# Moving the pool branch of each pass's first block into the key/query stage, with later group projections, spaced mix norms and held-back x loads

## The chip, the cores and the metric

The kernel runs as one program on all 8 cores of one Trainium2 chip (two dies of four cores). Each core computes 2048 tokens of a sequence and recomputes a halo block of 512 tokens in front of them. The time of a run is the device time of the slowest core, in microseconds (us). The four fast runs of the kernel before lie within 0.2% (1667.71 to 1671.0 us). Some executions fall into a slower state, in which the cores of one die, sometimes of both, show a lower mean granted TensorE clock: 0.81 to 0.93 in the slow runs, against 0.968 to 0.995 in profiled fast runs. A median below is that of the fast runs. In the traces of the kernel before, the clock records hold full and half clock alone. Matmuls of 512 columns start 0.214 us apart in gapless stretches at full clock and 0.43 us apart at half clock.

In this document PE is TensorE, DVE is VectorE, ACT is ScalarE, POOL is GpSimd and SP is SyncE. L179, L185 and so on are lines of the kernel. They are the lines of small helpers, so one line stands for many operations:

- L179 matmul, L185 and L186 activation (without and with a bias operand);
- L189 tensor-tensor, L194 scalar-tensor-tensor, L196 the same with an accumulated sum;
- L201 tensor-scalar, L209 copy or cast, L212 memset, L215 load or store.

## The reference

A macaron block: a SwiGLU feed-forward network (FFN), a token mixer with two gated branches, and a second FFN. Shift, scale and gate of each come from a conditioning vector through `w_ada`.

```python
def token_mix(h, w_in, ...):
    z = h @ w_in
    q, k, v, u, ga, gb = jnp.split(z, ...)          # 512, 512, 512, 512, 1024, 1024 columns
    ya = chunk_band_attention(q, k, v, ...) @ w_attn_out   # RMS norm of q and k per head, 8 heads
    yb = multiscale_pool(u, w_group, scale) @ w_pool_out   # trailing means of 2, 4, 8, 16 frames
    return (sigmoid(ga) * ya + sigmoid(gb) * yb) @ w_o

def multiscale_pool(u, w_group, scale):
    ...                                             # per group g: trailing mean minus u itself
    y = einsum('bsgc,gcd->bsgd', mixed, w_group)    # the group projection, 128x128 per group
    return y * scale
```

## The kernel before

Each core handles five blocks of 512 tokens, block 0 being the halo. The order of stages is: start (norms of blocks 0 and 1, `w_ada` dots), first FFN, then twice (a pass for blocks 1 and 2, another for 3 and 4) a key/query stage, attention and gates, then the second FFN. Matmuls run at bf16; weight loads other than `w_ada` cast from f32 on the way and are issued by POOL. SP issues `w_ada` and x.

**The filler.** In the key/query and attention stages, matmuls use what ScalarE makes of earlier ones (squares, logarithms, exponentials). `Fill` holds generators of other matmul work, for PE to run meanwhile, and feeds them in by credit. With it, PE's waits for ScalarE come to 2.3 us in the first key/query stage and 1.5 us in the first attention pass (core 4 of the kernel before). One credit is about one matmul of 512 columns.

```python
class Fill:
    def later(self, n, fn):            # run fn when n more credits of fill have passed
        self.late.append([n, fn])
    def run(self, n):
        self.credit += n
        while self.gens and self.credit > 0:
            try:
                c = next(self.gens[0]); self.credit -= c; self._passed(c)
            except StopIteration:
                self.gens.popleft()
        ...
```

**The fill work.** A value job has four tiles of 8 matmuls with two casts each. A pool job has four groups. Each group is 8 matmuls, a copy, 1 to 4 shifted adds on VectorE, and a subtraction. The group projection (one matmul and a scale, `yp`) comes 10 credits later. Both jobs take turns in two PSUM banks through `fbank`.

```python
    def fbank():
        fb[0] += 1
        return bank(4 + fb[0] % 2)

    def v_job(b, pas):
        for t in range(4):
            bk = fbank()
            ...                                        # 8 matmuls, yield 2 after each pair
            for o in range(2): ... P.copy(dst, src[:, :, o, :])        # L209, VectorE
            yield 2

    def u_job(b, pas, fill, in_a):
        def yp(g):
            bk = fbank()
            P.mm(bk, WPG[:, g, :], MIXED[g % 3][:, :], True, True)
            P.ts(yb_[:, g, :], bk, CST[:, 106 + g:107 + g], ALU.mult)  # L201, VectorE
        for g in range(4):
            bk = fbank()
            ...                                        # 8 matmuls
            u = UB[g % 2]
            if in_a: P.act(u[:, 16:528], bk, AF.Copy)  # first block of the pass: ScalarE
            else:    P.copy(u[:, 16:528], bk)          # second block: VectorE
            yield 2
            for st in range(g + 1):
                P.tt(dst[:, lo:528], src[:, lo:528], src[:, lo - sh:528 - sh], ALU.add)
                yield 0.5
            P.stt(MIXED[g % 3][:, :], src[:, 16:528], 1.0 / (2 << g), u[:, 16:528], ALU.mult, ALU.subtract)
            ...
            fill.later(10, lambda g=g: yp(g))
            yield 0.5
```

**The schedule.** `kq_seq(items, pas, fill, lead)` makes keys or queries: per half item, 16 matmuls, a square on ScalarE, `fill.run(lead)`, two matmuls for the head norms, then Ln, Exp and one VectorE operation. `attention(pas, fill, rate)` makes 40 steps (8 groups of 5, each group ending in a softmax denominator) and runs about `rate` credits of fill per step, less two for each value product.

```python
        if pas == 0:
            fill.add(v_job(0, pas))
            kq_seq([("K", 0)], pas, fill, 6)
            for t in tl: t.drain()                     # what is left of the mix norms
            fill.add(v_job(1, pas))
            kq_seq([("K", 1), ("Q", 1)], pas, fill, 6)
            kq_seq([("K", 2)], pas, fill, 6)
            release(("K", 0, pas), ("K", 1, pas))      # loads the U weights
            fill.add(u_tail(pas))
            fill.add(u_job(b1, pas, fill, True))
            kq_seq([("Q", 2)], pas, fill, 6)
        else: ...                                      # v_job(3), K3 K4, u_job(3), Q3 Q4, leads of 6
        fill.run(6)
        fill.add(v_job(b2, pas))
        fill.add(u_job(b2, pas, fill, False))
        attention(pas, fill, 5.0)
```

**The tail of the first FFN** (its last output projection) makes the mix norms of blocks 0 to 2. `tail_1(b, n)` is called after each of four output projections of a block and steps a queue of norm groups after three of them.

**The start.** SP queues x of blocks 2 to 4 (2 MB each) right behind the start's `w_ada` loads. POOL loads the first FFN's w1i pieces when certain `w_ada` dots are done. The first unit of four (a unit is 16 matmuls: one 128-column slice of the hidden layer for one block) overlaps the dots.

## Time and profile before

The median before was 1668.5 us (1667.71 to 1671.0 in three runs). The profiled execution spans 1667.4 us on its slowest core, core 4.

First the page. The lines of part 2 cut the span into 40 slices of about 42 us, and each digit is a busy share in tenths. PEclk is the granted clock in tenths of full speed.

```profile
PE 1537.1 (92%) x7085; PEld 672.7 (40%) x7085; DVE 820.2 (49%) x1300; ACT 480.2 (29%) x615; POOL 95.7 (6%) x191
...
PE   1498999999999998898799998799999999999999
...
PEclk9799999999999998898899998799999999999999
...
PE 83%; DVE 5%; ACT 4%; DMA 4%; issue 3%; SPq 0%; DVEq 0%; ACTq 0%; POOL 0%
```

PE is the limit, and the chain of waits that ends last is 83% PE. So only stretches where PE is not at 9 can be gained. These are the start, slices 16 and 17 (the end of the first FFN), and slices 19, 20, 25 and 26, which hold the attention stages.

Next PE's waits in total (us, times, longest).

```profile
PE ps L179 <- ACT arena L185: 37.1, 23, 11.9
PE ps L179 <- ACT arena L186: 27.3, 9, 14.6
PE ps L179 <- DMA arena<-w1i: 16.0, 3, 6.8
PE ps L179 <- DVE arena L209: 15.6, 7, 4.1
PE ps L179 <- DVE arena L194: 14.4, 6, 4.1
PE ps L179 <- DVE arena L189: 7.8, 4, 3.4
PE ps L179 <- DVE arena L201: 6.9, 3, 3.3
```

The four DVE lines sum to 44.7 us, nearly all in the tail, key/query and attention stages.

Then PE's timeline at the start (start, length, instruction, and in brackets the idle time before it with what ended it).

```profile
59.94 0.59 PE L179 MATMUL ps<-arena 128*128 128x512 bf16 x2 [1.85 <-ACT arena L186]
65.26 3.41 PE L179 MATMUL ps<-arena 128*128 128x512 bf16 x8 [4.73 <-DMA arena<-w1i]
73.16 3.57 PE L179 MATMUL ps<-arena 128*128 128x512 bf16 x8 [4.49 <-DMA arena<-w1i]
83.49 21.79 PE L179 MATMUL ps<-arena 128*128 128x512 bf16 x88 [6.76 <-DMA arena<-w1i]
```

PE waits three times for w1i, whose loads share the DMA engines with 6 MB of x: on this core x lands at 63.1, 70.8 and 77.5 us, w1i at 65.1, 73.0 and 83.4 us, and the DMA engines' busy share from 60 to 80 us is 1.01.

In the tail, the same view shows waits for squares on ScalarE, and one that ends in VectorE. VectorE was itself waiting for the `w_ada` loads of its last dots (4.71, 0.40, 2.12 and 4.14 us, from 612.7 to 629.6 us).

```profile
632.60 19.84 PE L179 MATMUL ps<-arena 128*128 128x512 bf16 x78 [3.89 <-DVE arena L194]
654.38 0.59 PE L179 MATMUL ps<-arena 128*128 128x512 bf16 x2 [1.93 <-ACT arena L185]
...
670.70 1.53 PE L179 MATMUL ps<-arena 128*128 128x512 bf16 x3 [3.60 <-ACT arena L185]
```

In the first attention pass, every wait of note is for VectorE. (How its work stands in line: PE ended at 778.44 us, and the casts that it waited for began at 780.95, directly behind four operations of L189 that VectorE had itself begun only at 778.91, after 3.35 us of waiting for ScalarE.)

```profile
769.59 8.86 PE L179 MATMUL ps<-arena 128*128 128x512 bf16 x39 [3.35 <-DVE arena L189]
781.86 5.19 PE L179 MATMUL ps<-arena 128*128 128x512 bf16 x19 [3.41 <-DVE arena L209]
...
812.80 7.19 PE L179 MATMUL ps<-arena 128*128 128x512 bf16 x38 [3.27 <-DVE arena L201]
...
828.22 3.26 PE L179 MATMUL ps<-arena 128*128 128x512 bf16 x17 [4.15 <-DVE arena L194]
```

Last, the busy time by window for the first key/query stage (first line) and the first attention pass (second line). The columns are window and length, busy us of PE, PEld, DVE, ACT and POOL with their instruction counts, then granted clock, DMA share and GB/s.

```profile
688.10:747.70 59.60, 56.52 (x279) 24.40 (x276) 26.88 (x48) 34.64 (x36) 2.82 (x4) 0.97 0.19 30
747.70:837.30 89.60, 68.24 (x363) 25.25 (x362) 56.71 (x130) 54.25 (x67) 8.50 (x36) 0.85 0.04 6
```

In attention no engine is full, and the granted clock is 0.85: PE keeps stopping, and stretches at half clock follow (0.43 us from one matmul to the next, as at 771 us). In the key/query stage PE is nearly full.

### The profile page before, as it was taken

To read this page: it belongs to the slowest core of one execution; us is meant where nothing else is said; L and a number is where in the kernel's file an instruction comes from. 1 tells how busy PE (TensorE), PEld (TensorE's weight loads), DVE (VectorE), ACT (ScalarE), POOL (GpSimd) and SP (SyncE) were. 2 spreads that over 40 slices of the span, in tenths; PEclk is the share of its full clock that TensorE was granted. 3 is DMA by queue.
4 is the path that set the end of the run, shared out by engine and by line. 5 is a ranking of instruction groups with operands and counts; after the bars stand their busy time and mean duration, and the time that the engine had idled before them with its cause. 6 is when DMAs were issued, how large, how long until landed. Compare 5 with 4: busy or idle time off the path is not lost.

```text
span 1667.4 us, 20421 instructions; the slowest of 8 cores (1653.6 to 1667.4 us)
## 1 busy us (share of the span) xinstructions
PE 1537.1 (92%) x7085; PEld 672.7 (40%) x7085; DVE 820.2 (49%) x1300; ACT 480.2 (29%) x615; POOL 95.7 (6%) x191
## 2 busy tenths in 40 slices
PE   1498999999999998898799998799999999999999
PEld 0133444444444443342244432244434444444444
DVE  4446736447346346735745445645456161613416
ACT  3354010110110114655644165644150101011110
POOL 0101000010010000000011100001101000001000
PEclk9799999999999998898899998799999999999999
DMA  9923353161370353030054530044504313104005
GB/s 280 267 54 88 62 123 80 39 140 33 90 145 10 89 127 75 1 51 1 1 89 76 88 51 1 1 89 77 88 1 76 51 26 57 26 14 83 13 1 202
DMA packets 45938, 119.50 MB, mean 72 GB/s; under 512 B 4112, under 2 KB 4240, under 8 KB 45328
## 3 DMA queue, kind: packets, MB, share of 16 engines
q0 software_dynamic: 31152, 59.91, 21.8%
q1 hardware_dynamic: 14688, 58.30, 10.7%
q8 instruction: 60, 0.98, 0.2%
q14 instruction: 38, 0.31, 0.1%
HBM read 169.70 MB, written 8.39 MB: 107 GB/s over the span
## 4 chain that ended last, share of the span: by engine, by line
PE 83%; DVE 5%; ACT 4%; DMA 4%; issue 3%; SPq 0%; DVEq 0%; ACTq 0%; POOL 0%
PE ps L179 83%; ACT arena L185 3%; DMA arena<-w_ada 2%; DVE arena L189 2%; DVE arena L194 2%; DMA arena<-w1i 1%; DVE arena L196 1%; ACT arena L186 1%; SPq L215 0%; DVE arena L209 0%; ACT L185 0%; ACT L186 0%; DVE arena L201 0%; DVEq L173 0%; DVE arena L205 0%
## 5 line engine op out<-in xcount | busy, mean ns | idle before, releaser
L179 PE MATMUL ps<-arena 128*128 128x512 bf16 (+5 forms) x7085 | 1537.1, 380 | 126.4 <-ACT arena L185 37.1
L179 PEld LDWEIGHTS ps<-arena 128*128 128x128 bf16 (+1 forms) x7085 | 672.7, 99 | 990.3 <-issue 246.6
L185 ACT ACTIVATE arena<-ps 128x512 bf16<-128x512 f32 (+4 forms) x368 | 271.0, 745 | 911.1 <-PE ps L179 903.7
L189 DVE TENSOR_TENSOR arena<-arena,ps 128x512 bf16<-128x512 bf16 (+1 forms) x230 | 175.2, 762 | 560.8 <-PE ps L179 493.3
L194 DVE SCALAR_TENSOR_TENSOR arena<-ps,arena 128x512 f32<-128x512 f32 (+1 forms) x410 | 315.5, 774 | 155.3 <-PE ps L179 80.2
L185 ACT ACTIVATE arena<-arena 128x1024 bf16<-128x1024 f32 (+2 forms) x105 | 95.2, 929 | 37.5 <-PE ps L179 15.8
L196 DVE SCALAR_TENSOR_TENSOR arena<-arena 128x1024 f32<-128x1024 f32 x72 | 87.8, 1220 | 32.4 <-DMA arena<-w_ada 18.3
L189 DVE TENSOR_TENSOR arena<-arena 128x512 bf16<-128x512 bf16 (+9 forms) x191 | 89.9, 494 | 27.0 <-ACT arena L185 19.6
L186 ACT ACTIVATE arena<-arena 128x512 bf16<-128x512 f32 (+1 forms) x84 | 57.5, 715 | 124.8 <-DVE arena L194 103.1
L194 DVE SCALAR_TENSOR_TENSOR arena<-arena 128x512 f32<-128x512 f32 (+2 forms) x114 | 78.9, 728 | 1.9 <-ACT arena L186 0.5
L215 POOL DMA_DIRECT2D arena<-w1i x26 | 17.1, 660 | 520.0 <-PE ps L179 470.2
L189 DVE TENSOR_TENSOR arena<-ps,arena 64x512 bf16<-64x512 f32 x32 | 22.0, 688 | 43.4 <-ACT arena L185 43.0
L215 POOL DMA_DIRECT2D arena<-w3i x24 | 16.3, 678 | 380.3 <-PE ps L179 380.3
L215 POOL DMA_DIRECT2D arena<-w_in x28 | 19.8, 707 | 297.3 <-PE ps L179 297.3
L186 ACT ACTIVATE arena<-ps,arena 128x1024 f32<-128x1024 f32 (+1 forms) x32 | 29.6, 926 | 17.4 <-PE ps L179 17.2
L185 ACT ACT_TABLE_LOAD x14 | 18.0, 1283 | 43.7 <-PE ps L179 36.5
L201 DVE TENSOR_SCALAR arena<-arena 128x512 bf16<-128x512 f32 (+2 forms) x45 | 19.8, 441 | 6.0 <-DMA arena<-cst 1.0
L212 POOL MEMSET arena<- 64x128 bf16 x64 | 11.9, 198 | 166.8 <-ACT arena L185 166.8
L186 ACT ACT_TABLE_LOAD x12 | 15.4, 1283 | 13.4 <-PE ps L179 13.3
L201 DVE TENSOR_SCALAR arena<-ps,arena 128x512 bf16<-128x512 f32 (+2 forms) x25 | 15.6, 638 | 4.6 <-PE ps L179 4.4
L209 DVE CAST arena<-ps 128x256 bf16<-128x256 f32 x32 | 12.0, 418 | 4.3 <-PE ps L179 4.0
L215 POOL DMA_DIRECT2D arena<-w_o x8 | 5.6, 704 | 73.8 <-PE ps L179 73.8
(14 smaller groups left out, 51.5 us busy)
## 6 DMA issues: line engine op xcount, KB each, us to landing
arena<-w_ada SPq DMA_DIRECT2D x72, 512.0 KB, 4.3
arena<-w_in POOLq DMA_DIRECT2D x28, 512.0 KB, 6.1
arena<-w3i POOLq DMA_DIRECT2D x20, 512.0 KB, 6.3
arena<-w1i POOLq DMA_DIRECT2D x18, 512.0 KB, 10.0
outT<-arena SPq DMA_DIRECT2D x16, 512.0 KB, 3.0
arena<-xT SPq DMA_DIRECT2D x3, 2048.0 KB, 23.0
arena<-w1o POOLq DMA_DIRECT2D x10, 512.0 KB, 16.5
arena<-w3o POOLq DMA_DIRECT2D x10, 512.0 KB, 9.6
```

The source lines that it names most:

```text
L179: return self.op("pe", lambda e: e.matmul(out, lhsT=lhsT, rhs=rhs, start=start, stop=stop), reads=[lhsT, rhs], writes=[out])
L185: return self.op("act", lambda e: e.activation(out=out, in_=in_, func=func, scale=scale), r, [out])
L186: return self.op("act", lambda e: e.activation(out=out, in_=in_, func=func, bias=bias, scale=scale), r, [out])
L189: return self.op(eng, lambda e: e.tensor_tensor(out=out, in0=in0, in1=in1, op=op), [in0, in1], [out])
L194: return self.op("dve", lambda e: e.scalar_tensor_tensor(out=out, in0=in0, scalar=scalar, in1=in1, op0=op0, op1=op1), r, [out])
L196: return self.op("dve", lambda e: e.scalar_tensor_tensor(out=out, in0=in0, scalar=scalar, in1=in1, op0=op0, op1=op1, accum_out=accum), r, ...
L201: return self.op(eng, lambda e: e.tensor_scalar(out=out, in0=in0, scalar1=s1, scalar2=None, op0=op0), r, [out])
L209: return self.op(eng, lambda e: e.tensor_copy(out=out, in_=in_), [in_], [out])
L212: return self.op(eng, lambda e: e.memset(out, v), [], [out])
L215: return self.op(q, lambda e: e.dma_start(out=out, in_=in_), [], [out], deps, sem)
```

## The change

The intent has five parts:

1. Start: hold the x of blocks 2 to 4 back until the first FFN's second w1i chunk has landed, and issue the w1i pieces at earlier dots. Put the `w_ada` dots of the first group in its last three blocks.
2. Tail: step the norm queue after every output projection, with empty groups that space a norm's matmuls from its squares.
3. Key/query stage: do the whole pool branch of the pass's first block there, with larger leads. The U weights are loaded before the Q weights. In the first pass the norms of blocks 1 and 2 are stepped inside.
4. Group projections 30 credits behind instead of 10, with four mix buffers. The projection takes the bank that the next job will use, without advancing the counter.
5. Attention: rate 4 instead of 5. Value tiles and pool groups of the second block alternate.

```diff
-            fill.later(10, lambda g=g: yp(g))
+            fill.later(30, lambda g=g: yp(g))
 ...
-            bk = fbank()
-            P.mm(bk, WPG[:, g, :], MIXED[g % 3][:, :], True, True)
+            bk = bank(4 + (fb[0] + 1) % 2)
+            P.mm(bk, WPG[:, g, :], MIXED[g][:, :], True, True)
 ...                                                   # first pass
+            tl[0].drain()
             fill.add(v_job(0, pas))
-            kq_seq([("K", 0)], pas, fill, 6)
-            for t in tl: t.drain()
-            fill.add(v_job(1, pas))
-            kq_seq([("K", 1), ("Q", 1)], pas, fill, 6)
-            kq_seq([("K", 2)], pas, fill, 6)
-            release(("K", 0, pas), ("K", 1, pas))
+            kq_seq([("K", 0)], pas, fill, 10, hook)
+            tl[1].drain()
             fill.add(u_tail(pas))
             fill.add(u_job(b1, pas, fill, True))
-            kq_seq([("Q", 2)], pas, fill, 6)
+            fill.add(v_job(1, pas))
+            kq_seq([("K", 1)], pas, fill, 10, hook)
+            tl[2].drain()
+            kq_seq([("K", 2)], pas, fill, 11)
+            release(("K", 0, pas), ("K", 1, pas))
+            kq_seq([("Q", 1), ("Q", 2)], pas, fill, 11)
 ...                                                   # second pass: leads 9, v and u alternate
-        fill.run(6)
-        fill.add(v_job(b2, pas))
-        fill.add(u_job(b2, pas, fill, False))
-        attention(pas, fill, 5.0)
+        for k in range(4):
+            fill.add(u_job(b2, pas, fill, False, [k]) if k < 2 else v_job(b2, pas, [k]))
+            fill.add(v_job(b2, pas, [k]) if k < 2 else u_job(b2, pas, fill, False, [k]))
+        fill.run(10)
+        attention(pas, fill, 4.0)
 ...                                                   # tail
+        for t in tl: t.step()                          # now after all four n
+                for k in (2, 1): ng.insert(k, [])
 ...                                                   # start
-                      [(0, 1), (2, 3)], (4, 5), startup=[dots[2], dots[11]], ...
+                      [(0, 1), (2, 3)], (4, 5), startup=[dots[1], dots[7], dots[11], dots[13]], ...
+    last = pre1()
+    P.load("sp", XB[1][:, :, :], xT[2], "d_x2", deps=last)      # then w_ada, then x of blocks 3 and 4
```

More of the change, by code (lines that the diff above doesn't have):

```diff
@@ L365, in build_nc @@
     TT = [view(o_h + 2112, F32, (528,)), view(o_h + 4224, F32, (528,))]
-    MIXED = [view(o_h + 6336, BF16, (TB,)), view(o_w + 4096 * 9 + 2112, BF16, (TB,)), view(base - 4096, BF16, (TB,))]
+    MIXED = [view(o_h + 6336, BF16, (TB,)), view(o_w + 4096 * 9 + 2112, BF16, (TB,)), view(base - 4096, BF16, (TB,)),
+             view(base - 2048, BF16, (TB,))]
     SG = [view(o_h + 4096 * i, F32, (2, TB)) for i in range(2)]
@@ L523, in build_nc @@
             early(b, kt)
-    for i in range(2):
-        ada_load(16 + i, ada_slot(16 + i), "d_b%d" % i)
-    for b in range(2, 5):
-        P.load("sp", XB[b - 1][:, :, :], xT[b], "d_x%d" % b)
     ada_j = [16]
@@ L558, in wi_load @@
             if split is not None:
-                for jj in range(nt):
-                    for s, o in ((sa, 0), (sb, NJ)):
-                        P.load("pool", piece(s)[:, jj:jj + 1, :],
+                return [P.load("pool", piece(s)[:, jj:jj + 1, :],
                                w_i[o + j0 + jj:o + j0 + jj + 1].rearrange("j p c -> p j c"),
-                               "d_w%d" % s if jj == 0 else "d_wy%d" % s, deps=[split[jj]])
-                return
+                               "d_w%d" % s if jj == 0 else "d_wy%d" % s, deps=[split[2 * k + jj]])
+                        for jj in range(nt) for s, o in ((sa, 0), (sb, NJ))]
             for s, o in ((sa, 0), (sb, NJ)):
@@ L612, in pre @@
         def pre():
-            wi_load(startup)
+            return wi_load(startup)
         def body():
-            wi_load()
+            if startup is None:
+                wi_load()
             wo_load(0)
@@ L681, in g0_1 @@
         g0_norms(4 * bi + u, N1)
-        if bi >= 1 and u % 2 == 0:
+        if bi >= 2 and u < 3:
             ada_step()
@@ L697, in tail_1 @@
     def tail_1(b, n):
+        for t in tl:
+            t.step()
         if n == 6:
@@ L708, in tail_1 @@
                     ng.append([lambda: P.copy(HT[:, :, :], H[0][:, :, TB - 16:TB])])
+                for k in (2, 1):
+                    ng.insert(k, [])
                 tl[b].q.extend(ng)
-            return
-        for t in tl:
-            t.step()
     pre1, body1 = ffn(w1i, w1o, 0, [0, 1, 2, 3, 4], True, dict(g0=g0_1, g0end=g0end_1, unit=unit_1, op=lambda: None),
-                      [(0, 1), (2, 3)], (4, 5), startup=[dots[2], dots[11]], tail=tail_1,
+                      [(0, 1), (2, 3)], (4, 5), startup=[dots[1], dots[7], dots[11], dots[13]], tail=tail_1,
                       spread=lambda kt: warm(5) if 2 <= kt <= 6 else None)
     pre1()
+    last = pre1()
+    P.load("sp", XB[1][:, :, :], xT[2], "d_x2", deps=last)
+    for i in range(2):
+        ada_load(16 + i, ada_slot(16 + i), "d_b%d" % i)
+    for b in range(3, 5):
+        P.load("sp", XB[b - 1][:, :, :], xT[b], "d_x%d" % b)
     P.load("pool", WPG[:, :, :], w_pg.rearrange("(g c) d -> c g d", c=128), "d_wpg", deps=[dots[15]])
@@ L759, in build_nc @@
     for p_ in range(2):
-        for k in ("K", "V", "Q", "U"):
+        for k in ("K", "V", "U", "Q"):
             wq.extend([(k, 0, p_), (k, 1, p_)])
@@ L767, in build_nc, with kq_seq @@
     flag = CST[:, 110:111]
-    def kq_seq(items, pas, fill, lead):
+    def kq_seq(items, pas, fill, lead, hook=None):
         n_ = 0
@@ L780, in kq_seq @@
                 P.act(SQK[i], pair(i), AF.Square)
+                if hook is not None:
+                    hook()
                 fill.run(lead)
@@ L797, in fbank, with v_job @@
         return bank(4 + fb[0] % 2)
-    def v_job(b, pas):
+    def v_job(b, pas, tiles=range(4)):
         sl = SLOT[b]
-        for t in range(4):
+        for t in tiles:
             bk = fbank()
@@ L833, in u_tail, with u_job @@
         yield 4
-    def u_job(b, pas, fill, in_a):
+    def u_job(b, pas, fill, in_a, gs=range(4)):
         yb_ = YP[(b - 1) % 2]
         def yp(g):
-            bk = fbank()
-            P.mm(bk, WPG[:, g, :], MIXED[g % 3][:, :], True, True)
+            bk = bank(4 + (fb[0] + 1) % 2)
+            P.mm(bk, WPG[:, g, :], MIXED[g][:, :], True, True)
             P.ts(yb_[:, g, :], bk, CST[:, 106 + g:107 + g], ALU.mult)
-        for g in range(4):
+        for g in gs:
             bk = fbank()
@@ L864, in u_job @@
                 yield 0.5
-            P.stt(MIXED[g % 3][:, :], src[:, 16:528], 1.0 / (2 << g), u[:, 16:528], ALU.mult, ALU.subtract)
+            P.stt(MIXED[g][:, :], src[:, 16:528], 1.0 / (2 << g), u[:, 16:528], ALU.mult, ALU.subtract)
             if b == 1:
@@ L868, in u_job @@
                 P.tt(t16[:, 0:16], src[:, 16:32], CST[:, 112 + 16 * g:128 + 16 * g], ALU.mult)
-                P.tt(MIXED[g % 3][:, 0:16], t16[:, 0:16], u[:, 16:32], ALU.subtract)
-            fill.later(10, lambda g=g: yp(g))
+                P.tt(MIXED[g][:, 0:16], t16[:, 0:16], u[:, 16:32], ALU.subtract)
+            fill.later(30, lambda g=g: yp(g))
             yield 0.5
@@ L976, in build_nc, with hook @@
         if pas == 0:
-            v_ones(0)
-            fill.add(v_job(0, pas))
-            kq_seq([("K", 0)], pas, fill, 6)
-            for t in tl:
-                t.drain()
-            v_ones(1)
-            v_ones(2)
-            fill.add(v_job(1, pas))
-            kq_seq([("K", 1), ("Q", 1)], pas, fill, 6)
-            kq_seq([("K", 2)], pas, fill, 6)
-            release(("K", 0, pas), ("K", 1, pas))
+            def hook():
+                for t in tl[1:]:
+                    t.step(2)
+            tl[0].drain()
+            for b in range(3):
+                v_ones(b)
+            fill.add(v_job(0, pas))
+            kq_seq([("K", 0)], pas, fill, 10, hook)
+            tl[1].drain()
             fill.add(u_tail(pas))
             fill.add(u_job(b1, pas, fill, True))
-            kq_seq([("Q", 2)], pas, fill, 6)
+            fill.add(v_job(1, pas))
[4 more added lines that the diff above has]
+            kq_seq([("Q", 1), ("Q", 2)], pas, fill, 11)
         else:
@@ L993, in build_nc @@
             v_ones(4)
-            fill.add(v_job(3, pas))
-            kq_seq([("K", 3), ("K", 4)], pas, fill, 6)
+            for k in range(4):
+                fill.add(v_job(3, pas, [k]))
+                fill.add(u_job(b1, pas, fill, True, [k]))
+            kq_seq([("K", 3), ("K", 4)], pas, fill, 9)
             release(("K", 0, pas), ("K", 1, pas))
-            fill.add(u_job(b1, pas, fill, True))
-            kq_seq([("Q", 3), ("Q", 4)], pas, fill, 6)
+            kq_seq([("Q", 3), ("Q", 4)], pas, fill, 9)
         release(("Q", 0, pas), ("Q", 1, pas))
-        fill.run(6)
-        fill.add(v_job(b2, pas))
-        fill.add(u_job(b2, pas, fill, False))
-        attention(pas, fill, 5.0)
+        for k in range(4):
+            fill.add(u_job(b2, pas, fill, False, [k]) if k < 2 else v_job(b2, pas, [k]))
+            fill.add(v_job(b2, pas, [k]) if k < 2 else u_job(b2, pas, fill, False, [k]))
+        fill.run(10)
+        attention(pas, fill, 4.0)
         release(("V", 0, pas), ("V", 1, pas), ("U", 0, pas), ("U", 1, pas))
```

## The prediction

> **What bounds the kernel now.** TensorE. The page gives it 92% busy; its 7085 recorded matmuls, at the 0.214 us per 512-column matmul of the gapless stretches, fill at most 1464 us of the 1667 us span. The chain of waits is 83% PE. Stages where PE idles matter; in 20 us windows and PE's timeline:
>
> 1. Start: PE runs gaplessly only from 152 us. Units 2 to 4 of the first block wait for w1i (4.7, 4.5, 6.8 us); the last piece, issued at 59.5, lands at 83.4, behind 6 MB of x issued at 47 us. They also run at half clock (0.43 us per matmul).
> 2. End of the first FFN: DVE waits for the last w_ada dots (617 to 631 us); PE idles 3.9 us, then runs 16 matmuls at half clock.
> 3. The tail with mix norms (640 to 706 us): PE idles 1.9, 3.6, 0.8 and 2.3 us, mostly for squares, half clock following.
> 4. Attention, 748 to 838 and about 1000 to 1087 us. A group of five steps takes 13 us while pool-branch work fills it, 7.6 us with value-projection fill, 6.8 us without (denominators in ScalarE's timeline). PE there waits 2 to 4 us for VectorE (casts L209, scale L201, L189, L194). No engine is full; VectorE's in-order chain costs, with the group projection only 10 matmuls behind it.
>
> [...] Here gaps of 1.9 to 3.9 us are followed by 0.43 us matmuls, so a removed gap counts nearly double.
>
> **What the change does.** No arithmetic goes; work moves.
> - x loads wait for the second w1i chunk, which is issued at dots 11 and 13 (51 and 55 us), so should land near 61 us. Unit 4 starts near 68 us, not 83.5. Given back: the later blocks' x lands at 73 to 90, so ScalarE's squares stall a little. Net -12 us.
> - Ada dots leave the second block, three in each later block: neutral there, but the last comes one unit earlier: -5 us.
> - Spaced norm groups in the tail: -9 us of idle and slow clock.
> - First pass: about 50 fill matmuls move from attention into the key/query stage, gapless on PE from 707 to 748 us: +10.6 us there. Second pass: about 28, +6 us.
> - Attention: the fill falls from about 112 and 88 to 62 matmuls, pool groups alternate with value tiles, and the group projection comes 30 matmuls later. ScalarE then bounds it: 40 exponentials of 1.02 us (1.1 apart) plus eight denominators of 1.8 us, 58 us a pass. Expected: 65 to 68 us against 87 and 84: -21 and -17 us.
>
> Sum: -12 -5 -9 +10.6 +6 -21 -17 = -47; a little goes to new waits.
>
> **Predicted: 1623 us, 1604 to 1643 with 80%.** Faster by over 2%: 0.80; within 2%: 0.19; slower: 0.01.
>
> **Right if:** no PE wait for w1i near 83 us, and gapless PE begins near 140 us; no half-clock stretch at 632 us; key/query stages longer; attention groups of 7.5 to 9 us instead of 12 to 13; PE's waits for L209/L201/L194 nearly gone (30 us before).
>
> **Wrong if:** held-back x makes ScalarE hold up the SiLUs behind its squares, so the start gains little; query weights, now loaded only after key weights are released, arrive late; or attention stays bound by latency, PE at half clock for want of fill.

(The mark stands for a sentence that was cut, since nothing in this case shows the rule it gave for the clock. No term of the sum went with it: -12 -5 -9 +10.6 +6 -21 -17 = -47.4, put there as -47. That a removed gap counts nearly double is the author's estimate, from matmuls 0.43 us apart instead of 0.214 behind gaps of core 4. The landing times of w1i (61 us) and of the later x (73 to 90 us) are the author's estimates too, and so are the 1.1 us between exponentials: in the kernel before they start 0.90 us apart or more, for example at 792.23, 793.13, 794.03 and 795.21 us on core 4.)

## The result, and the profile after

The changed kernel took 1639.03 us in the median (1637.44 to 1643.42, four runs), against 1668.4 us before. The ratio is 0.9825 with a 95% interval of 0.9803 to 0.9847. A ratio is the mean time of one kernel's fast runs over that of the other's of the same rounds, so it is not quite the ratio of the quoted medians. The kernel is clearly faster, by 1.75%. That is short of the 2% which would count as "faster".

The page of the slowest core (core 3, span 1638.0 us):

```profile
PE 1517.3 (93%) x7085; PEld 669.1 (41%) x7085; DVE 821.3 (50%) x1300; ACT 478.9 (29%) x615; POOL 96.2 (6%) x193
...
PE   1488999999999999988699988799999999999999
...
PEclk9899999999999999999999999899999999999999
...
PE 82%; ACT 5%; DVE 5%; DMA 4%; issue 3%; SPq 0%; DVEq 0%; ACTq 0%; POOL 0%; POOLq 0%
```

PE's waits:

```profile
PE ps L179 <- ACT arena L185: 55.6, 35, 12.0
PE ps L179 <- ACT arena L186: 29.5, 10, 17.5
PE ps L179 <- DVE arena L201: 10.9, 5, 3.9
PE ps L179 <- DVE arena L209: 7.3, 4, 3.0
PE ps L179 <- DMA arena<-w_ap: 5.9, 2, 3.4
PE ps L179 <- DVE arena L189: 5.9, 6, 2.4
PE ps L179 <- DVE arena L194: 0.6, 1, 0.6
```

The waits for w1i are gone and the DVE waits fell from 44.7 to 24.7 us. The wait for the scale (L201) grew from 6.9 to 10.9 us, the wait for ScalarE (L185) grew by 18.5 us, and a wait for `w_ap` is new on this core. Where those new waits lie is visible in PE's timeline.

```profile
62.65 7.50 PE L179 MATMUL ps<-arena 128*128 128x512 bf16 x34 [0.83 <-ACT arena L186]
82.11 8.15 PE L179 MATMUL ps<-arena 128*128 128x512 bf16 x30 [11.96 <-ACT arena L185]
...
646.25 0.59 PE L179 MATMUL ps<-arena 128*128 128x512 bf16 x2 [2.75 <-ACT arena L185]
...
724.89 2.32 PE L179 MATMUL ps<-arena 128*128 128x512 bf16 x10 [3.24 <-DVE arena L201]
...
760.18 4.94 PE L179 MATMUL ps<-arena 128*128 128x512 bf16 x17 [3.04 <-DVE arena L209]
```

At the start there is one gap of 12 us on this core where there were three for w1i. ScalarE's timeline says what it was doing in that time:

```profile
66.64 1.08 ACT L185 ACTIVATE arena<-ps 128x512 bf16<-128x512 f32 x2
80.91 2.00 ACT L185 ACTIVATE arena<-arena 128x1024 bf16<-128x1024 f32 x2 [13.19 <-DMA arena<-xT]
82.82 0.58 ACT L185 ACTIVATE arena<-ps 128x512 bf16<-128x512 f32 x1
```

It stood before the squares of block 2, which need the held-back x. PE waits for these squares themselves: the norm statistics of block 2, four matmuls over squares, stand in PE's stream before the fourth unit. On all eight cores PE starts again 0.14 to 0.15 us after the first square ends. The SiLU of the third unit, whose matmuls had ended at 70.15, stood in line behind the squares too (the line at 82.82), but the fourth unit uses the PSUM pair of the first, whose SiLU had run at 66.64. (Some expectations below place this gap before the fifth unit; it lies before the fourth.)

The windows of the first key/query stage and the first attention pass:

```profile
672.50:743.90 71.40, 64.40 (x316) 28.39 (x314) 40.74 (x83) 36.98 (x40) 2.81 (x4) 0.98 0.20 30
743.90:812.50 68.60, 53.04 (x318) 20.23 (x318) 42.03 (x93) 51.64 (x63) 7.50 (x35) 0.93 0.00 1
```

The attention pass has 45 matmuls less (363 to 318), VectorE lost 14.7 us of work in it, and it took 68.6 us instead of 89.6. The key/query stage took 71.4 us instead of 59.6.

The slowest core differs from run to run, so the experiments below are read by stage, as means over all eight cores of each profile. The bounds in the first FFN are the ends of SiLUs on ScalarE, one for each unit: the 4th, the 20th (end of the first group) and the 110th (the last output projection follows). Matmuls can't be counted there, because two cores of before and two of after lack 140 matmul records in their traces. The later bounds are the first key matmul (taken as 3.6 us before the first square of keys), the first attention matmul, and the last narrow one. This table was worked out from the traces in that way.

| stage, mean of 8 cores, us | before | after | difference | predicted |
|---|---|---|---|---|
| to the end of the fourth unit | 91.1 | 82.4 | -8.7 | |
| rest of the first group | 71.6 | 73.0 | +1.4 | the two: -12 |
| rest of the first FFN | 457.3 | 457.3 | 0.0 | |
| tail | 59.9 | 55.7 | -4.2 | -5 and -9 |
| key/query stage, first pass | 59.1 | 71.4 | +12.3 | +10.6 |
| attention, first pass | 88.8 | 69.6 | -19.2 | -21 |
| gates, first pass | 114.5 | 114.9 | +0.4 | |
| key/query stage, second pass | 43.9 | 53.3 | +9.4 | +6 |
| attention, second pass | 89.7 | 67.1 | -22.6 | -17 |
| rest | 583.3 | 583.6 | +0.3 | |
| span | 1659.4 | 1628.4 | -31.0 | -47 |

The same traces say what the 31.0 us consist of. In the mean of the cores PE's idle time fell by 15.6 us (129.5 to 113.9), and the time in which PE ran at half clock fell by 30.7 us (72.9 to 42.2), which is 15.4 us of work at full clock.

The start is the least steady of these stages. In the runs whose start code is that of the change, the first group ends between 155.4 and 158.6 us (155.4 in the change's own profile), so differences of 3 us there say nothing.

### The profile page after: what moved, and what is told of

It reads as the page before. It is cut to its first block, busy times and chain, and to the rows that moved or that the text cites. A ratio compares the mean times of both kernels' runs of the same rounds, so it can differ in the third digit from the quotient of the medians.

```text
span 1638.0 us, 20449 instructions; the slowest of 8 cores (1622.4 to 1638.0 us)
## 1 busy us (share of the span) xinstructions
PE 1517.3 (93%) x7085; PEld 669.1 (41%) x7085; DVE 821.3 (50%) x1300; ACT 478.9 (29%) x615; POOL 96.2 (6%) x193
## 4 chain that ended last, share of the span: by engine, by line
PE 82%; ACT 5%; DVE 5%; DMA 4%; issue 3%; SPq 0%; DVEq 0%; ACTq 0%; POOL 0%; POOLq 0%
PE ps L179 82%; ACT arena L185 3%; DVE arena L189 2%; DVE arena L194 1%; DMA arena<-w_ada 1%; ACT arena L186 1%; DMA arena<-w_ap 1%; DMA arena<-xT 1%; DVE arena L196 1%; SPq L215 0%; DMA arena<-w1i 0%; DVE arena L209 0%; DVE arena L201 0%; ACT L185 0%; ACT L186 0%
## 5 line engine op out<-in xcount | busy, mean ns | idle before, releaser
L179 PE MATMUL ps<-arena 128*128 128x512 bf16 (+3 forms) x7085 | 1517.3, 377 | 116.8 <-ACT arena L185 55.6
L185 ACT ACTIVATE arena<-ps 128x512 bf16<-128x512 f32 (+4 forms) x368 | 270.3, 744 | 870.5 <-PE ps L179 862.1
L194 DVE SCALAR_TENSOR_TENSOR arena<-ps,arena 128x512 f32<-128x512 f32 (+1 forms) x410 | 315.8, 774 | 125.6 <-PE ps L179 71.1
L185 ACT ACTIVATE arena<-arena 128x1024 bf16<-128x1024 f32 (+2 forms) x105 | 95.2, 929 | 42.8 <-DMA arena<-xT 17.6
L189 DVE TENSOR_TENSOR arena<-arena 128x512 bf16<-128x512 bf16 (+10 forms) x191 | 89.9, 494 | 25.5 <-ACT arena L185 17.3
L194 DVE SCALAR_TENSOR_TENSOR arena<-arena 128x512 f32<-128x512 f32 (+2 forms) x114 | 78.8, 727 | 6.2 <-ACT arena L186 2.9
L201 DVE TENSOR_SCALAR arena<-arena 128x512 bf16<-128x512 f32 (+2 forms) x45 | 19.9, 443 | 5.7 <-DMA arena<-cst 1.1
L186 ACT ACT_TABLE_LOAD x12 | 15.4, 1283 | 16.3 <-PE ps L179 16.2
L201 DVE TENSOR_SCALAR arena<-ps,arena 128x512 bf16<-128x512 f32 (+2 forms) x25 | 15.7, 644 | 7.2 <-PE ps L179 7.0
L209 DVE CAST arena<-ps 128x256 bf16<-128x256 f32 x32 | 12.1, 419 | 7.4 <-PE ps L179 7.4
L209 DVE COPY arena<-arena 128x16 f32<-128x16 f32 (+2 forms) x35 | 6.0, 171 | 8.2 <-ACT arena L185 6.8
```

What stands on the lines that cost most here:

```text
L179: return self.op("pe", lambda e: e.matmul(out, lhsT=lhsT, rhs=rhs, start=start, stop=stop), reads=[lhsT, rhs], writes=[out])
L185: return self.op("act", lambda e: e.activation(out=out, in_=in_, func=func, scale=scale), r, [out])
L186: return self.op("act", lambda e: e.activation(out=out, in_=in_, func=func, bias=bias, scale=scale), r, [out])
L189: return self.op(eng, lambda e: e.tensor_tensor(out=out, in0=in0, in1=in1, op=op), [in0, in1], [out])
L194: return self.op("dve", lambda e: e.scalar_tensor_tensor(out=out, in0=in0, scalar=scalar, in1=in1, op0=op0, op1=op1), r, [out])
L201: return self.op(eng, lambda e: e.tensor_scalar(out=out, in0=in0, scalar1=s1, scalar2=None, op0=op0), r, [out])
```

## The experiments

All twelve kernels gave correct results. The runs of one call (1 to 4; 5 to 8; 9 to 11; 12) share their runs of the kernel before. Times of different calls come from different chips, so their ratios are compared as well.

### 1. The start put back

```diff
-    P.load("sp", XB[1][:, :, :], xT[2], "d_x2", deps=last)   # and the rest of the change's start
+    for b in range(2, 5):                                    # behind the last w_ada loads, as before
+        P.load("sp", XB[b - 1][:, :, :], xT[b], "d_x%d" % b)
-startup=[dots[1], dots[7], dots[11], dots[13]]
+startup=[dots[2], dots[11]]
-        if bi >= 2 and u < 3:
+        if bi >= 1 and u % 2 == 0:
```

> The change with its start put back: x loads, w1i pieces and ada dots as in the kernel before. Costing of the prediction: the start is worth 12 us (and 5 more at the end of the first FFN on the core that waited there), so 1651 to 1656 us. Reading of the two traces over all cores: the fourth unit starts 10.5 us earlier but the norms of the first group give 3.2 us back, so about 1646 us. Rival: on the slowest core the wait for w1i was only swapped for a wait for x (12 us for the squares), so no more than 4 us, 1640 to 1643 us.

Measured: 1647.15 us, ratio 0.9858 (0.9837 to 0.9879). The fourth unit is done at 93.4 us instead of 82.4 in the mean, and the first group at 165.7 instead of 155.4. The tail is 58.9 us in the mean instead of 55.7, because two cores stand at 65.5 and 67.1 us: the wait that VectorE ends (L194, behind the last `w_ada` dots) is back there with gaps of 6.64 and 6.88 us, and on no other core. The start is worth about 8 us in the time. That falls short of the prediction's costing (-12 and -5) and fits the reading over all cores (about 1646 us).

### 2. The tail put back as it was, without spacing

```diff
-        for t in tl:                    # at the head of tail_1
-            t.step()
-                for k in (2, 1):
-                    ng.insert(k, [])
+            return                      # no step after the fourth output projection
+        for t in tl:
+            t.step()
```

> The change with the mix norms of the tail stepped as in the kernel before (three groups per block, no empty ones). Costing of the prediction: the spacing is worth 9 us, so 1648 us, with gaps of 1.9 and 3.6 us before the norm matmuls and half-clock matmuls after them. Reading of the traces: the tail lost one gap of the two and kept one of 2.75 us, so 3 to 4 us, 1643 us. Rival: the gain there was the removed ada wait alone, so 1639 us.

Measured: 1639.59 us, ratio 0.9808 (0.9791 to 0.9825). The time is that of the change. By stage the tail is 58.7 us instead of 55.7, and the gaps of 1.93 and 3.60 us are back as expected. The key/query stage is 1.4 us longer and the following attention 1.7 us shorter. So the spacing removes about 3 us in the tail's own stage, and no gain in the time could be shown (the first group also ended 2.1 us later in this run, which is chance). The prediction's 9 us for it is wrong.

### 3. Projection early, everything else as changed

```diff
-            fill.later(30, lambda g=g: yp(g))
+            fill.later(10, lambda g=g: yp(g))
```

> The change with the group projection 10 matmuls behind its pool group instead of 30; all else as changed. Theory that lateness is what freed attention: groups with pool work go back to 11 to 13 us, each attention pass from 68 to about 80 us, time 1655 to 1662 us. Rival, that moving the first block's pool branch out and alternating pool groups with value tiles freed it: passes stay below 73 us, time 1639 to 1645 us.

Measured: 1657.08 us, ratio 0.9911 (0.9891 to 0.993). The time fell into the range of the first theory, but for another reason. The attention passes took 72.0 and 69.9 us, only 2.4 and 2.8 us more than with the change, so they stayed nearly free. The loss is in the key/query stages: 82.6 us instead of 71.4 and 56.3 instead of 53.3. PE's timeline in the first of them (core 2) shows how:

```profile
716.23 8.40 PE L179 MATMUL ps<-arena 128*128 128x512 bf16 x27 [4.66 <-DVE arena L209]
727.50 7.67 PE L179 MATMUL ps<-arena 128*128 128x512 bf16 x27 [2.86 <-DVE arena L201]
737.51 3.77 PE L179 MATMUL ps<-arena 128*128 128x512 bf16 x10 [2.34 <-DVE arena L201]
```

The late projection is what makes it cheap to put the pool branch into the key/query stage. It is not what freed attention.

### 4. The work back in attention, projection late

Here the key/query and attention stages are scheduled as in the kernel before (shown above under its schedule), with leads of 6, rate 5 and no alternation. The late projection, four mix buffers and the bank rule stay.

```diff
-        attention(pas, fill, 4.0)       # and the schedule of the change before it
+        attention(pas, fill, 5.0)       # and the schedule of the kernel before
-        for k in ("K", "V", "U", "Q"):
+        for k in ("K", "V", "Q", "U"):
```

> The opposite corner: key/query and attention stages scheduled as in the kernel before (pool branch of the first block mostly in attention, query weights before pool weights, leads of 6, rate 5, no alternation), but the projection 30 behind, four mix buffers and the new bank rule kept. Key/query stages should shrink by 12 and 9 us in both theories. If lateness alone frees attention, passes take 72 to 76 us and the kernel is as fast as the change or faster, 1626 to 1636 us. If the move and the alternation free it, passes go back to 85 to 90 us and the time is 1655 to 1662 us.

Measured: 1652.38 us, ratio 0.9883 (0.9866 to 0.99). The attention passes are 90.2 and 89.6 us, as in the kernel before (88.8 and 89.7), although projections are late. The key/query stages are 57.0 and 43.3 us. The schedule of the change, given late projections, costs 14.4 and 10.0 us there, and it wins 20.6 and 22.5 us in attention. So the schedule is what freed attention. Three things differ in it: the move, the rate and the alternation. The runs 8 to 10 separate these.

### 5. The bank rule put back

```diff
-            bk = bank(4 + (fb[0] + 1) % 2)
+            bk = fbank()
```

> The change with the group projection taking the next fill bank and advancing the counter again, as before the change; all else as changed. If the new rule (projection and next job share a bank) is what makes the new waits of 3.2 and 3.9 us for the scale L201 in the key/query stages, these vanish: stages 68 and 49.5 us, time 1632 us. If the rule helps, because otherwise the next job waits for the bank of a job whose copy stands behind the projection's scale, stages and attention grow: 1642 to 1648 us.

Measured: 1646.74 us, ratio 0.9872 (0.9849 to 0.9896). The first key/query stage is 74.5 us (+3.1), the second 55.0 (+1.7), and the second attention pass 72.5 (+5.4). The rule helps. The first theory was right about the waits for the scale, though: without the rule PE's waits for L201 fall from 10.9 to 2.1 us (slowest core, 0). But those for casts and copies, L209, rise from 7.3 to 22.0:

```profile
PE ps L179 <- DVE arena L209: 22.0, 11, 4.5
PE ps L179 <- DVE arena L201: 2.1, 2, 1.5
```

So the rule exchanges one wait for a larger one that it removes.

### 6. Held-back x in four pieces

```diff
-    P.load("sp", XB[1][:, :, :], xT[2], "d_x2", deps=last)
+    for p in range(4):
+        P.load("sp", XB[1][:, 2 * p:2 * p + 2, :], xT[2][:, 2 * p:2 * p + 2, :], "d_x2%d" % p, deps=last)
```

> The change with the held-back x of the third block loaded in four pieces of 512 KB, in the order in which its squares read them; all else as changed. If ScalarE's wait for the whole 2 MB is what cost the start (PE gaps of 4.5 to 12 us before the fifth unit), the fourth unit starts 4 to 8 us earlier on the slow cores and the time is 1631 to 1635 us. If the transfers as a whole are the limit, the same time is lost later in the first group, waiting for the x of the fourth and fifth block: 1637 to 1640 us.

Measured: 1639.37 us, ratio 0.9829 (0.98 to 0.9857). The fourth unit is done at 84.6 us in the mean (82.4 with the change) and the first group at 156.5 (155.4), which is no gain. On core 3 the gap of 11.96 us is now two:

```profile
75.85 1.01 PE L179 MATMUL ps<-arena 128*128 128x512 bf16 x2 [6.37 <-ACT arena L185]
79.50 15.86 PE L179 MATMUL ps<-arena 128*128 128x512 bf16 x63 [2.64 <-ACT arena L185]
```

The single gap became shorter, but nothing is gained at the end of the group. The time is that of the rival, but the place is not: the loss does not move to the later blocks. In the mean the fourth unit itself is done no earlier, since ScalarE now waits for the later pieces as well (7.60, 2.59 and 0.91 us on core 3). The size of the load is not the limit.

### 7. The first block's projection scale on ScalarE

```diff
-            P.ts(yb_[:, g, :], bk, CST[:, 106 + g:107 + g], ALU.mult)
+            if in_a:
+                P.act(yb_[:, g, :], bk, AF.Identity, scale=CST[:, 106 + g:107 + g])
+            else:
+                P.ts(yb_[:, g, :], bk, CST[:, 106 + g:107 + g], ALU.mult)
```

> The change with the scale of the first block's group projections (the one in the key/query stages) on ScalarE instead of VectorE. If VectorE's chain ahead of that scale is the new wait, the gaps of 3.2 and 3.9 us go, key/query stages become 68 and 49.5 us and the time 1631 to 1634 us. Rival: ScalarE is the engine that squares, logarithms and exponentials wait for, so its 0.6 us each come back as waits for squares, 1637 to 1641 us.

Measured: 1632.83 us, ratio 0.979 (0.9767 to 0.9813). The key/query stages are 69.6 and 50.7 us (-1.8 and -2.6). The first stage's gap of 3.24 us shrank to 1.63 and is now ended by ScalarE (core 2):

```profile
718.78 2.32 PE L179 MATMUL ps<-arena 128*128 128x512 bf16 x10 [1.63 <-ACT arena L185]
```

The theory is right in kind. VectorE's chain of shifted adds stood between the projection and its scale (2.30 us of adds from 721.78, the scale at 724.00, on core 3 of the change), while PE's next job wanted that bank. The rival is right about part of it, since a wait for ScalarE remains.

### 8. No alternation in attention

```diff
-        for k in range(4):
-            fill.add(u_job(b2, pas, fill, False, [k]) if k < 2 else v_job(b2, pas, [k]))
-            fill.add(v_job(b2, pas, [k]) if k < 2 else u_job(b2, pas, fill, False, [k]))
+        fill.add(v_job(b2, pas))
+        fill.add(u_job(b2, pas, fill, False))
```

> The change without the alternation in attention: the second block's four value tiles, then its four pool groups, at the same rate of 4; the first block's pool branch stays in the key/query stage. If the move alone freed attention, passes stay at 66 to 72 us and the time at 1637 to 1642 us. If alternation does a good part, groups with pool work take 12 us again and passes 75 to 80 us, time 1650 to 1660 us.

Measured: 1626.78 us, ratio 0.9752 (0.9729 to 0.9774), faster than the kernel before. Neither theory expected it: the alternation is a loss of 6.1 and 3.9 us a pass (63.5 and 63.2 us without it). Of PE's waits, those for the casts and copies L209 go from 7.3 us to this (slowest core, 7; in the two attention passes, over all cores, from 6.4 us in the mean to none):

```profile
PE ps L179 <- DVE arena L209: 0.2, 1, 0.2
```

That is the wait of 3.04 us seen at 760.18 in the change, and its like in the second pass. With alternation a value tile is issued between two pool groups. That its cast stands on VectorE behind a pool group's adds while PE wants its bank is the likely reading of those lines, but no run took that cast away by itself. Without alternation, groups of five steps that hold fill take 6.8 to 7.2 us (core 2, first pass). ScalarE is busy for 6.5 to 6.6 us of each, so they are near ScalarE's limit.

### 9. No alternation, and the fill spread to the end

```diff
-        attention(pas, fill, 4.0)
+        attention(pas, fill, 3.4)       # on top of experiment 8
```

> The change without alternation and with attention's fill rate at 3.4 instead of 4, so that the fill of about 62 matmuls lasts over all eight groups. Against the run without alternation alone (1626.8 us, passes 63.5 and 63.2 us, last three groups 8 to 9.3 us with gaps of 2.4 us and half clock, filled ones 7.2): if the unfilled end is the loss, all groups take 7 to 7.3 us, passes 59 to 60 us, time 1618 to 1621 us. If the end of each group waits for the denominator whatever is filled in, passes stay at 63 us and the time at 1625 to 1628 us.

Measured: 1633.74 us, ratio 0.977 (0.9733 to 0.9807). Only three of its four runs were fast, and they lie 6.1 us apart (1630.42 to 1636.56). The passes did fall, to 60.9 and 61.1 us, but the first gates stage grew from 115.7 to 119.0 us and the rest, which holds the second gates, by 5.1. PE's timeline behind the first pass (core 2) shows what fills it:

```profile
805.90 0.38 PE L179 MATMUL ps<-arena 128*128 128x512 bf16 x1 [1.01 <-DVE arena L201]
807.28 4.91 PE L179 MATMUL ps<-arena 128*128 128x512 bf16 x22 [1.01 <-DVE arena L201]
```

These are three group projections, 30 credits late, which now come due after attention (531 matmuls in the gates stage instead of 528) and are drained one by one through one bank. Each waits for the scale of the one before. The expected 6 to 9 us did not come. What attention gained was given back there.

### 10. The work back in attention, at a lower rate

```diff
-        attention(pas, fill, 5.0)
+        attention(pas, fill, 4.0 if pas else 4.6)     # on top of experiment 4
```

> The run with the work back in attention (1652.4 us, passes 90.2 and 89.6 us), with only the rate lowered, from 5 to 4.6 in the first pass (the least that places all fill) and 4 in the second. If the density of pool work per step is what clogs VectorE, and not the amount of it in attention, the second pass falls from 89.6 to 72 to 78 us although it holds all 88 fill matmuls, and the first by a few us: time 1634 to 1643 us. If the move itself is what counts, passes stay above 84 us and the time at 1647 to 1653 us.

Only two of its four runs were fast: 1651.44 and 1653.58 us. By stage (from a fast profile), the second pass took 80.1 us instead of 89.6, and the first 87.5 instead of 90.2. That is between the two theories. For the second pass the runs add up: the lower rate takes 9.5 us away, and the move (with its leads and its order of weights) 16.9 more, down to the 63.2 us of experiment 8, which has the same rate of 4 and no alternation. The alternation gives 3.9 back, which leaves the 22.5 us between experiment 4 and the change.

Outside attention most of the lower rate's gain is paid again. The first gates took 118.6 us instead of 114.4, more than the 2.7 us that the first pass gained, and the rest, with the second gates, 589.0 instead of 582.7. The two fast times are no better than those of experiment 4 (1649.04 to 1653.49 us).

### 11. The first w1o loads held back

```diff
-            wo_load(0)
+                if startup is not None and bi == 1:
+                    wo_load(0, [done])                # done: last product of block 1's units
```

> The change with the first two w1o loads (1 MB read each, issued beside the held-back x) held until the second block's units of the first group are done; nothing needs them before about 150 us. If what delays x is the traffic beside it, the third block's x lands some 6 us earlier, PE's gap before the fifth unit (4.5 to 12 us) shrinks to 0 to 5 us, fourth unit at 72 us in the mean of the cores instead of 77, time 1632 to 1635 us. If x alone fills that time, nothing changes: 1637 to 1640 us; worse if w1o then comes late for the first output projection.

Measured: 1637.04 us, ratio 0.979 (0.9766 to 0.9815). Over the eight cores the x of block 2 now lands 8.8 to 11.1 us after its issue instead of 9.2 to 15.3 (1.5 us less in the mean), and the slowest core's fourth unit is done at 84.9 us instead of 87.4. The mean does not move (82.6 against 82.4), but x was also issued 1.4 us later in this run (65.7 against 64.3). A gap of 4.9 to 7.7 us stays. So w1o explains the worst cores and not the whole gap. What is left is x's own transfer, or that of the x of blocks 3 and 4, which are issued 1 to 4 us behind it; no run separates these two. The 2 us in the time are inside the intervals.

### 12. What the runs point to, together

The change without alternation, at rate 3.4, with the scale of experiment 7 and the held w1o of experiment 11.

> What the runs point to, together: the change without alternation, fill rate 3.4, the first block's projection scale on ScalarE and the first w1o loads held back. Stage sums from the runs, taken from the change: passes of attention from 69.6 and 67.1 to about 61 each, key/query stages from 71.4 and 53.3 to 70 and 51, the start's slowest core 2 us earlier: 1639 - 15 - 4 - 2 = 1618 us, 1614 to 1624 us, ratio to the kernel before 0.968 to 0.973. If the gains do not add, because the scale on ScalarE stands in the way of its exponentials or the held w1o comes late, 1625 to 1632 us.

Measured: 1616.73 us in the median of five fast runs (four between 1615.71 and 1619.42, one at 1637.95), ratio 0.9717 (0.9668 to 0.9765), faster than the kernel before. It also beats the change, whose ratio is 0.9825 on other rounds. The key/query stages take 70.0 and 50.7 us and attention 60.5 and 59.9, and the cores lie within 4.5 us of each other. The total met the expectation, in part by luck, for its terms did not all: the rate's gain is again paid in the gates (118.1 us and, in the rest, 586.0 instead of 583.6). In the mean of the cores the gain over the change is 16.0 us and not 21. The slowest core gained more, because the cores had lain 15.6 us apart in the change's profile. A version with rate 4 and the other three edits was not run.

## Why the prediction was right or wrong

The record forecast 1623 us (1604 to 1643), and 1639 us were measured, so the range held. The chance of 0.80 for a gain over 2% did not come true: the ratio was 0.9825. The sum of steps was -47 us against -31.0 in the mean of the cores and -29.4 in the slowest. The move, key/query and attention stages together, came out as costed: -20.1 us against -21.4. Most of what is missing is in the start and the tail: -11.5 us against -26.

- **What bounds the kernel: right.** The named stages are the ones that moved. The rest of the first FFN and the stages behind the second attention pass did not change (0.0 and +0.3 us).
- **Attention, -21 and -17: right in size** (-19.2 and -22.6), in part by luck, as the causes below show. The limit named, ScalarE, is neared only once alternation is out (experiment 8). In the change the groups took 6.8 to 11.4 us in core 3's first pass, not 7.5 to 9, and PE's waits for L209, L201 and L194 fell from 36.9 to 18.8 us and were not nearly gone. **Its causes were wrong in two of three.** The later projection is worth only 2.4 and 2.8 us in attention (experiment 3), and it does nothing there without the new schedule (experiment 4). The alternation, counted as help, costs 6.1 and 3.9 us (experiment 8). What freed attention is the first block's pool branch moved out (16.9 us in the second pass), together with the lower rate (9.5 us there, most of it paid again behind the pass; experiments 4, 8 and 10).
- **Key/query stages, +10.6 and +6: the size short** by 1.7 and 3.4 us, **because the work did not stay gapless.** They measured +12.3 and +9.4. The stages hold 37 and 24 matmuls more, not about 50 and 28; at 0.214 us each that is 7.9 and 5.1 us. The rest is mostly idle time of PE, which waits 3.24 and 3.91 us for the projection's scale behind a pool group's adds. About half of that goes when the scale runs on ScalarE (experiment 7).
- **Start, -12 net: mis-sized.** The gain from earlier w1i was right: the unit that waited for it until 83.49 us on core 4 (the third; the record calls it the fourth) starts at 66.2 us instead of 81.8 in the mean of the cores, 15.6 us earlier against the record's 15.5. But the fourth unit was done only 8.7 us earlier, and 1.4 us more were given back in the group, so the net is -7.3. The step that failed is "so ScalarE's squares stall a little". The squares stalled for 13.19 us on core 3, and PE, whose own stream holds matmuls over them, for 4.5 to 12 us by core. The start is worth about 8 us in the time (experiment 1). The record's first reason for being wrong came close to this, but named the SiLUs behind the squares and not the squares.
- **The last ada dot, -5: mis-sized.** It was read from core 4 alone. The gap of 3.89 us before the matmul at 632.60 is on none of the other seven cores of that profile, and in experiment 1 its like is on two of eight. In the mean of the cores it is therefore worth well under 5 us. In the metric it weighs more: core 4 was the slowest in that profile, and the two cores of experiment 1 were the slowest there (1651.2 and 1649.0 us).
- **Spaced norm groups, -9: mis-sized, the largest failure.** The tail as a whole fell by 4.2 us, with the ada wait included. Undoing the spacing cost 3.0 us in the stage and nothing measurable in the time (experiment 2). One gap of 3.60 us went, but another of 1.93 became one of 2.75. In both kernels its squares stand on ScalarE behind the eight exponentials of the bias table (3.29 us, from 641.88 to 645.17, on core 3 of the change; eight of 0.49 us on core 4 before), and spacing matmuls from squares does not touch that. This is read from ScalarE's timeline; no run moved the exponentials.
- **"A removed gap counts nearly double": right in the sum, not gap by gap.** In the mean of the cores 15.6 us less idle time came with a gain of 31.0 us, the other half being matmuls that no longer ran at half clock (30.7 us less time at half clock). The prediction put that price on every gap, its author's estimate, and gap by gap it does not hold. In the kernel before, matmuls at 0.43 us do follow the gaps of 1.93, 3.60 and 3.89 us on core 4, and in the change one of 2.01 us on core 3. After the gap of 3.24 us in the change, core 3 ran on at 0.21 us, while core 2 had nine matmuls at half rate after a gap of the same length. So a single gap between 2 and 4 us had no fixed price here.
- **Query weights late: did not happen.** PE never waits for `w_in`. A late weight appears elsewhere: `w_ap`, loaded when attention releases its weights, made core 3's PE wait 2.48 and 3.40 us behind the two passes. It is hardly the change's doing: in the mean of the cores PE waits 1.9 us for `w_ap`, and waited 1.5 us before.

Open: why the alternation costs what it does is read from waits and not isolated. The split between move and rate is from one profile by stage. What makes the x of block 2 late, its own transfer or the x queued behind it, is not separated.

## What to carry to other kernels

Filler work has a price in its amount, its density and its order: 16.9, 9.5 and 3.9 us in this kernel's second attention pass. Check where the deferred work ends up, since most of what the lower density gained was paid again in the next stage. A load that is held back to clear the way for another should be checked for who reads it first, and for what stands behind that reader: here ScalarE stood for 13.19 us before the late squares on core 3, and PE for 4.5 to 12 us by core before matmuls over them. Read a stage over all cores before pricing a wait: two of the mis-sized terms came from the slowest core or from one gap alone.
